# Small products on zeros, a quartered input and a later residual at the head of a two-layer trunk

## The chip, the cores and the metric

The kernel runs on one core of a Trainium2 chip. Its time is the device time of one execution in microseconds (us); the metric is the median over several runs. A core has TensorE (PE: matrix products, with PEld as its weight loads), VectorE (DVE), ScalarE (ACT), GpSimd (POOL) and SyncE (SP, which only issues transfers here).

## The reference, cut to what matters

Two layers work on 256 prompt rows and 32 sample rows (8 batches of 4), each of 1024 features. A layer is a feed-forward half step, a mixing step and a second feed-forward half step, each followed by a residual sum and a layer norm:

```python
def swiglu(x, w_in, w_out):
    gate, up = jnp.split(x @ w_in, 2, axis=-1)
    return (jax.nn.silu(gate) * up) @ w_out
...
x = layer_norm(ALPHA * x + 0.5 * swiglu(x, p['ffn1_w_in'][l], p['ffn1_w_out'][l]), p['ln1_g'][l], p['ln1_b'][l])
z = x @ p['mix_w_in'][l]
...
x = layer_norm(ALPHA * x + mix, p['ln2_g'][l], p['ln2_b'][l])
x = layer_norm(ALPHA * x + 0.5 * swiglu(x, p['ffn2_w_in'][l], p['ffn2_w_out'][l]), p['ln3_g'][l], p['ln3_b'][l])
```

`ffn1_w_in` has 1024 rows and 2 x 2816 columns. Everything is float32. The mixing step (three groups of heads) is not touched by the change.

## The kernel before

All activations are held with features on the 128 partitions and the 288 tokens along the row: x is eight chunks of 128 x 288. To keep float32 accuracy on a faster form of product, each operand is split into a high part (rounded to the format that PE takes at full pace) and a low part (the rest), and a product is three: low weights by high x, high weights by high x, high weights by low x.

`load_x` (line 720) brings the input in. It comes in rows of tokens, in three tiles `xin` (128, 128 and 32 rows of 1024 features), each in two halves of the features, all issued by SP; after the loads of each half it calls `prep` for one block of weights. Then, for each of the eight chunks, PE transposes the three pieces into one PSUM tile `xps`, ACT makes the high part, DVE the low part, and ACT a copy times ALPHA into `ax`, the tile in which the residual sum is formed at the end of the feed-forward step.

`prep` (line 338) loads a block of up to four chunks by 256 columns (`raw`, three buffers), lets ACT make its high part `wh` and DVE its low part `wl` (three buffers each), with a priority of 250 instructions ahead of what was traced before. `weights` (line 359) keeps up to two blocks prepared ahead in the list `wr`. `dense_g` (line 390) forms one product of 256 columns from the blocks that `blocks` lists (chunks 0 to 3, then 4 to 7 for the 1024 features); `block` (line 374) issues the three products of each chunk, for two column halves: 24 products a block, 48 for 256 columns.

`ffn` (line 465) goes through eleven rounds, each a gate product and an up product of 256 columns; before round j it calls `mid[j]()`: in layer 0 the constants made on POOL (`consts`, round 0) and the small parameters (`params`, rounds 5 and 6). `post` (line 496) adds the output product to `ax` and forms the norm. The order of each engine's instructions comes from a scheduler that works by these priorities and by what is ready in its own model of time, so an instruction may stand well ahead of the place where the program has it; on the chip each engine takes its instructions in that fixed order, and so does SP its transfers.

Of the kernel before, what the change touches and what calls it, by code (L numbers as in the profile page):

```python
# [8 lines left out]
F32 = mybir.dt.float32  # L9
F32R = mybir.dt.float32r  # L10
BF16 = mybir.dt.bfloat16
# [6 lines left out]
DM = 1024  # L18
T = 256
# [19 lines left out]
class Trunk:  # L39
    def __init__(self, ctx, tc, I, O):  # L40
# [12 lines left out]
        self.dn, self.dshare, self.l = 0, False, 0  # L53

# [27 lines left out]
    @contextmanager  # L82
    def prio(self, n):
        """Work that the scheduler may issue ahead of what is traced before it."""
        v = PR.get(n, 0) + PR.get(f"{n}@{self.l}", 0)
        self.tc.cur_priority -= v
        yield
        self.tc.cur_priority += v
# [31 lines left out]
    def consts(self):  # L120
# [34 lines left out]
        # causal masks over [s, t]: t > s and t >= s  # L155
# [5 lines left out]
        # block-merge masks: ml[b][t, s] and mt[b][s, t]  # L161
# [13 lines left out]
        # the same for blocks of 64 tokens, in rows of (block parity, token)  # L175
# [19 lines left out]
        # sample block masks over [(h,s), (h,t)], blocks of four tokens  # L195
# [9 lines left out]
        # the same with the rows of head h at the place of head (h + 2) % 4  # L205
# [3 lines left out]
        # row -> batch within a 32-token group, and row -> parity of its head  # L209
# [10 lines left out]
        # sums over a head's 64 rows into 32 equal rows, and their spreading back  # L220
# [11 lines left out]
        # a token's row in each group of 32; minus one at odd rows  # L232
# [3 lines left out]
        # two heads' inclusive sample blocks in either half of the rows  # L236
# [17 lines left out]
        # a token's row in each group of 32, for either pair of heads  # L254
# [3 lines left out]
        # the first four rows repeated for each batch  # L258
# [3 lines left out]
        # token -> batch, and a token's row in each group of 32  # L262
# [4 lines left out]
        # reset points of the running sums: token 0 of each chunk  # L267
# [70 lines left out]
    def prep(self, spec):  # L338
        """A block of weights, loaded and split into high and low parts."""
# [19 lines left out]
    def weights(self, spec):  # L359
        """The prepared block; the next one in line is prepared before it is used."""  # L360
        if not self.wq or self.wq[0] != spec:
            return self.prep(spec)
        while len(self.wr) < 2 and len(self.wr) < len(self.wq):
            self.wr.append(self.prep(self.wq[len(self.wr)]))
        self.wq.pop(0)
        return self.wr.pop(0)
# [7 lines left out]
    def block(self, spec, x, res, first, last):  # L374
        """A block's share of a product."""
# [14 lines left out]
    def dense_g(self, w, n0, x, nk, pool, res):  # L390
        res += [self.dps() for _ in range(2)]
        bl = self.blocks(w, n0, nk, pool)
# [9 lines left out]
    def dense_by(self, w, n0s, x, groups):  # L402
        """Several products, each group of chunks through all of them before the next."""
# [7 lines left out]
    def fill(self, n=1):  # L411
        """Goes on with the products in the background by n steps."""
# [18 lines left out]
    def hilo(self, r, name, n=NT):  # L431
        """Rows of high and low parts in turn, of equal rows."""
# [5 lines left out]
    def newx(self, nt):  # L438
        """Operand tiles of a product's moving side: eight 128-row chunks, high and low parts."""
# [9 lines left out]
    def zfix(self, ps, st, nm):  # L449
        """A product's two column blocks, and their biases, with the norm's scale (and shift) applied."""  # L450
# [45 lines left out]
    def post(self, wout, x, nk, coef, ln, shift, groups=None):  # L496
        """Residual sum with a product, and its layer norm: the operand tiles of the next product hold
        (u - m) g in high and low parts, with m the mean of the first six chunks (shift) or of all."""
# [100 lines left out]
    def final(self, po, m6, coef, g, square, i):  # L599
        """The last norm, in rows of tokens, and the outputs; the last rows are the prompt's end and the samples."""  # L600
# [6 lines left out]
        def rows(j, c):  # L607
            """A chunk, times the norm's gain, in rows of tokens."""
# [40 lines left out]
        # the mean's rest as rows of high, low and high parts  # L649
# [34 lines left out]
    def final_load(self, l):  # L684
        """The last norm's shift in each row, and its gain in (negated) rows of high, high and low parts."""
# [10 lines left out]
    def residual_g(self, pend):  # L696
        """The norm's output itself, times ALPHA for the next residual sum."""
# [9 lines left out]
    def residual_x(self):  # L707
        """The same, and operand tiles of it."""
# [11 lines left out]
    def load_x(self, specs):  # L720
        """The operand tiles of the inputs; both loads in halves of the features, and the first weights between."""
        nc, I = self.nc, self.I
        rows = []
        xin = [self.m4([128, DM], f"xin{j}") for j in range(3)]
        self.wq += specs
        for hf in range(2):
            fs = slice(512 * hf, 512 * hf + 512)
            for j, r in enumerate(xin):
                if j < 2:
                    nc.sync.dma_start(r[:, fs], I["x_prompt"][0, j * 128:(j + 1) * 128, fs])  # L730
                else:
                    nc.sync.dma_start(r[:NS, fs], I["x_sample"].rearrange("b t d -> (b t) d")[:, fs])
            self.wr.append(self.prep(specs[hf]))
        x = self.newx(NT)
        for c in range(KC):
            p = self.ps(f"xps{c}")
            for j, r in enumerate(xin):
                n = 128 if j < 2 else NS
                self.tr(p[:, 128 * j:128 * j + n], r[:n, c * 128:(c + 1) * 128])
            self.act(x[0][c], p[:, :NT])  # L740
            self.sub(x[1][c], p[:, :NT], x[0][c].bitcast(F32))
            self.act(self.ax[:, c], p[:, :NT], scale=ALPHA)
        return x

# [43 lines left out]
    def rw_pre(self, l, q, zs):  # L788
# [3 lines left out]
        # lora products  # L792
# [3 lines left out]
        else:  # L796
            # tanh(x) = 2 sigmoid(2 x) - 1
# [19 lines left out]
        # running sums of the log decay (in units of -exp(-0.5)), centred in each chunk  # L817
# [17 lines left out]
        # keys  # L835
# [30 lines left out]
        # (sum r k r_k) v, and the norm's shift  # L866
# [13 lines left out]
    def gnorm(self, l, x, n):  # L880
        """Rows of tokens, less the means of n groups of 64, and one over each group's deviation."""
# [12 lines left out]
    def rw_gate(self, q, OT, p, G, BO, m, ts):  # L894
        """The norm's gain and shift, the bonus and the gate, into chunks 0 and 1 of the operand tiles m."""
# [33 lines left out]
    def rw_prompt(self, l, KR, bh, kh, V, eP, em):  # L929
        """Four chunks of 64 tokens; rows are (chunk parity, token), matrices [rows, chunk pair, head, token]."""  # L930
# [8 lines left out]
        # token-major values, first keys beside AT[1] in the order of its matrices, second keys  # L939
# [15 lines left out]
        def heads(j=None, i=None):  # L955
            """Chunk pair, parity, head pair, head, its rows, its columns and its matrix."""
# [7 lines left out]
        def pairs(name, f):  # L964
            """Products of both head parities, in turn in the array's two row halves."""
# [9 lines left out]
        for qi, src in ((0, bh), (2, kh)):  # L975
# [13 lines left out]
            if qi == 0:  # L989
                # the inverse over pairs of tokens, and its transpose  # L990
# [12 lines left out]
        # token-major values, keys and (negated) first operands  # L1003
# [15 lines left out]
        # inverses over twice as many tokens, from I - (the block between two halves) times the inverse  # L1019
# [25 lines left out]
        # corrections without the state, and their dependence on it  # L1045
# [11 lines left out]
        # from one chunk's state to the next, and to the outputs  # L1057
# [3 lines left out]
        # decay from a chunk's centre to its end, and on to the next chunk's centre  # L1061
# [36 lines left out]
        # token-major outputs  # L1098
# [31 lines left out]
    def rw_load(self, l):  # L1130
        nc, I = self.nc, self.I
        # carried states, rows (parity of the batch, value)
# [7 lines left out]
    def rw_sample(self, l, KR, bh, kh, V, eP):  # L1140
# [9 lines left out]
        # the carried states transposed to rows (head, key)  # L1150
# [8 lines left out]
        # keys and queries of each batch alone  # L1159
# [508 lines left out]
    def run(self):  # L1668
# [6 lines left out]
        def par(l):  # L1675
            return lambda: q.append(self.params(l))
# [156 lines left out]
```

## Time and profile before

| | us |
|---|---|
| median of 3 runs | 1374.07 |
| the three runs | 1373.8, 1374.07, 1381.42 |
| span of the profiled execution | 1379.8 |

The profiled execution's span is the time from its first to its last instruction on the core; PE is busy 1308.3 us of it (95%), DVE 1009.8, ACT 663.8, POOL 274.1. Matmuls are pipelined, so a busy PE is not one at its full pace: the distance between the starts of two products tells the pace. A row of the trace names the engine, the line of the kernel and the tiles (out <- in); "x7" means that seven such instructions are merged, and the time in front of it is from the first start to the last end. What stands in square brackets is the engine's idle time before the row and what ended it. "d" is the PSUM tile of the dense products, "xps" that of the transposes.

### The profile page before, as it was taken

What the parts mean: (1) busy time and instruction counts of PE and PEld (TensorE: products, weight loads), DVE (VectorE), ACT (ScalarE), POOL (GpSimd) and SP (SyncE); (2) the same over time, 40 slices, a digit from 0 to 9 for tenths busy, and PEclk for the clock granted to TensorE, in tenths of its full rate; (3) what the DMA queues carried; (4) which work ended last, traced back from release to release, by engine and by line L of the source; (5) the groups of instructions that cost most, each with busy time, mean ns of one, the idle gap of its engine ahead of it and who ended that gap; (6) DMA issues with size and microseconds to landing.
All of it is one profiled execution on the core that took longest, in us unless ns stands there. A gap on an engine that the chain in (4) does not pass through costs nothing.

```text
span 1379.8 us, 27635 instructions
## 1 busy us (share of the span) xinstructions
PE 1308.3 (95%) x11161; PEld 1255.1 (91%) x11162; DVE 1009.8 (73%) x1844; ACT 663.8 (48%) x1052; POOL 274.1 (20%) x381
## 2 busy tenths in 40 slices
PE   7999999898987999999999999998889889999998
PEld 6999999877876999999999999997778789999997
DVE  3555448977877998774698775599986889977643
ACT  4454435762345554443465443368333645544433
POOL 9200001435554100000100000033464421000002
PEclk9999999987997999999999999999999889999999
DMA  5655554531123655554455555554212544555551
GB/s 175 187 168 168 162 165 150 154 106 34 48 86 113 187 156 158 165 168 153 155 168 167 167 156 161 167 160 131 78 31 71 149 124 145 168 161 161 175 168 58
DMA packets 208158, 194.12 MB, mean 141 GB/s; under 512 B 15911, under 2 KB 206363, under 8 KB 208030
## 3 DMA queue, kind: packets, MB, share of 16 engines
q1 hardware_dynamic: 207326, 190.91, 44.9%
q0 software_dynamic: 608, 1.31, 0.4%
q8 instruction: 88, 1.44, 0.4%
q14 instruction: 40, 0.33, 0.1%
q10 hardware_dynamic: 96, 0.13, 0.1%
HBM read 185.10 MB, written 7.22 MB: 139 GB/s over the span
## 4 chain that ended last, share of the span: by engine, by line
PE 79%; DVE 14%; issue 3%; ACT 2%; POOL 1%; DMA 0%; POOLq 0%; SPq 0%; DVEq 0%; ACTq 0%
PE d L97 71%; DVE wl L65 2%; DVE hgO L77 1%; ACT wh L62 1%; DVE yrw L77 1%; DVE hgQ L77 1%; PE pA L97 1%; DVE hR L65 1%; DVE hAT L94 1%; PE hO L97 0%; PE hA L97 0%; DVE ax L65 0%; PE pD L97 0%; POOL hgP L65 0%; DVE hL L65 0%
## 5 line engine op out<-in xcount | busy, mean ns | idle before, releaser
L97 PE MATMUL d<-x,wh 128*128 128x290 f32 (+1 forms) x3968 | 824.0, 301 | 2.5 <-DVE x L77 2.5
L97 PEld LDWEIGHTS d<-x,wh 128*128 128x128 f32 x3968 | 653.3, 192 | 9.8 <-DVE x L77 4.3
L97 PE MATMUL d<-x,wl 128*128 128x290 f32 (+1 forms) x1984 | 602.5, 304 | 16.2 <-ACT x L62 12.4
L62 ACT ACTIVATE wh<-raw 128x1024 fp32r<-128x1024 f32 x344 | 357.2, 1039 | 456.1 <-PE d L97 312.1
L65 DVE TENSOR_TENSOR wl<-raw,wh 128x1024 fp32r<-128x1024 f32 x324 | 395.1, 1220 | 239.4 <-ACT wh L62 238.1
L97 PEld LDWEIGHTS d<-x,wl 128*128 128x128 f32 x1984 | 380.5, 192 | 21.5 <-ACT x L62 15.5
L97 PE MATMUL d<-h,wh 128*128 128x288 f32 x1408 | 282.0, 296 | 0.0
L97 PEld LDWEIGHTS d<-h,wh 128*128 128x128 f32 x1408 | 226.2, 188 | 0.2
L97 PE MATMUL d<-h,wl 128*128 128x288 f32 x704 | 207.8, 295 | 0.0
L65 POOL TENSOR_TENSOR lnv<-lnq,lnq 128x288 f32<-128x288 f32 x6 | 8.2, 1375 | 848.7 <-ACT lnq L62 848.7
L97 PEld LDWEIGHTS d<-h,wl 128*128 128x128 f32 x704 | 132.5, 188 | 0.2
L65 POOL TENSOR_TENSOR wl<-raw,wh 128x1024 fp32r<-128x1024 f32 x20 | 50.0, 2502 | 66.3 <-ACT wh L62 66.3
L62 ACT ACTIVATE h<-sg 128x288 fp32r<-128x288 f32 x88 | 38.1, 435 | 24.5 <-DVE sg L65 20.9
L62 ACT ACTIVATE sg<-yg,ccg 128x288 f32<-128x288 f32 x66 | 34.3, 528 | 29.9 <-DVE yg L77 29.9
L62 ACT ACT_TABLE_LOAD x37 | 47.5, 1283 | 1.4 <-PEq L1821 0.8
L65 DVE TENSOR_TENSOR h<-sg,h 128x288 fp32r<-128x288 f32 x88 | 39.6, 452 | 5.6 <-ACT h L62 5.6
L77 DVE SCALAR_TENSOR_TENSOR ax<-d,ax 128x288 f32<-128x288 f32 x48 | 21.4, 452 | 29.4 <-PE d L97 29.4
L77 DVE SCALAR_TENSOR_TENSOR yu<-nu,ccu,yu 128x288 f32<-128x288 f32 x66 | 33.9, 514 | 0.8
L77 DVE SCALAR_TENSOR_TENSOR yg<-nu,ccg,yg 128x288 f32<-128x288 f32 x66 | 33.8, 515 | 0.8
L62 ACT ACTIVATE lnq<-ax 128x288 f32<-128x288 f32 x48 | 20.9, 435 | 26.2 <-DVE ax L77 26.0
L77 DVE SCALAR_TENSOR_TENSOR sg<-yu,ccu,sg 128x288 f32<-128x288 f32 x66 | 33.3, 509 | 0.0
L65 DVE TENSOR_TENSOR yu<-d,rho 128x288 f32<-128x288 f32 x66 | 29.5, 448 | 0.0
(499 smaller groups left out, 1355.2 us busy)
## 6 DMA issues: line engine op xcount, KB each, us to landing
raw<-in_ffn_w_in SPq DMA_DIRECT2D x176, 512.0 KB
raw<-in_ffn_w_out SPq DMA_DIRECT2D x80, 512.0 KB
raw<-in_mix_w_in SPq DMA_DIRECT2D x56, 512.0 KB
raw<-in_mix_w_out SPq DMA_DIRECT2D x12, 512.0 KB
raw<-in_ffn_w_out SPq DMA_DIRECT2D x16, 256.0 KB
hs<-in_state_hgrn SPq DMA_DIRECT2D x8, 512.0 KB
out_hgrn_state_sample<-hs SPq DMA_DIRECT2D x8, 512.0 KB
raw<-in_mix_w_out SPq DMA_DIRECT2D x8, 256.0 KB
```

The costliest lines, as they stand in the source:

```text
L62: self.nc.scalar.activation(out, in_, func, **kw)
L65: (eng or self.nc.vector).tensor_tensor(out, a, b, op=op)
L77: self.nc.vector.scalar_tensor_tensor(out, a, s, b, op0=op0, op1=op1)
L94: self.nc.vector.copy_predicated(out, mask.bitcast(I16), data)
L97: self.nc.tensor.matmul(out, lhsT, rhs, start=start, stop=stop)
```

## The change

Five things are changed. PE gets 14 products (128 x 128 by 128 x 288, 16-bit) on a tile of zeros before anything else, into a PSUM tile that nobody reads. The prompt's x is loaded in quarters of the features, both 128-row tiles in one transfer, by SP; the samples' quarters are issued by ACT. The first weight column is loaded in three blocks (chunks 0 and 1, 2 and 3, 4 to 7) in place of two, one after each of the first three quarters, and `dense_g` takes that list for the first product. The ACT copies times ALPHA are gone from `load_x`. In their place `residual_0`, called before round 4 of the first feed-forward step, adds the high and the low part of each chunk on POOL into `ax` and scales it by ALPHA on ACT. The rest of the diff takes away comments and is left out here.

```diff
-        self.dn, self.dshare, self.l = 0, False, 0
+        self.dn, self.dshare, self.l, self.head = 0, False, 0, None
...
     def dense_g(self, w, n0, x, nk, pool, res):
         res += [self.dps() for _ in range(2)]
-        bl = self.blocks(w, n0, nk, pool)
+        bl, self.head = self.head or self.blocks(w, n0, nk, pool), None
...
-    def load_x(self, specs):
+    def load_x(self, w):
         nc, I = self.nc, self.I
-        rows = []
-        xin = [self.m4([128, DM], f"xin{j}") for j in range(3)]
-        self.wq += specs
-        for hf in range(2):
-            fs = slice(512 * hf, 512 * hf + 512)
-            for j, r in enumerate(xin):
-                if j < 2:
-                    nc.sync.dma_start(r[:, fs], I["x_prompt"][0, j * 128:(j + 1) * 128, fs])
-                else:
-                    nc.sync.dma_start(r[:NS, fs], I["x_sample"].rearrange("b t d -> (b t) d")[:, fs])
-            self.wr.append(self.prep(specs[hf]))
+        wt = self.ep.tile([128, NT], BF16, tag="e", name="warm", bufs=B["e"])
+        nc.vector.memset(wt, 0.0)
+        p = self.ps("warmps")
+        for _ in range(WARM):
+            self.mm(p[:, :NT], wt[:, 0:128], wt)
+        xp = [self.m4([128, 2, 512], f"xin{j}") for j in range(2)]
+        xs = self.m4([128, DM], "xins")
+        ks = ((0, 1), (2, 3), tuple(range(4, 8)))
+        self.head = [(*w, k, 0, False) for k in ks]
+        self.wq += self.head
+        for f in range(4):
+            fs = slice(256 * f, 256 * f + 256)
+            nc.sync.dma_start(xp[f // 2][:, :, 256 * (f % 2):256 * (f % 2) + 256],
+                              I["x_prompt"][0, :, fs].rearrange("(j p) f -> p j f", p=128))
+            nc.scalar.dma_start(xs[:NS, fs], I["x_sample"].rearrange("b t d -> (b t) d")[:, fs])
+            if f < 3:
+                self.wr.append(self.prep(self.head[f]))
         x = self.newx(NT)
         for c in range(KC):
             p = self.ps(f"xps{c}")
-            for j, r in enumerate(xin):
-                n = 128 if j < 2 else NS
-                self.tr(p[:, 128 * j:128 * j + n], r[:n, c * 128:(c + 1) * 128])
+            for j in range(2):
+                self.tr(p[:, 128 * j:128 * j + 128], xp[c // 4][:, j, 128 * (c % 4):128 * (c % 4) + 128])
+            self.tr(p[:, T:NT], xs[:NS, c * 128:(c + 1) * 128])
             self.act(x[0][c], p[:, :NT])
             self.sub(x[1][c], p[:, :NT], x[0][c].bitcast(F32))
-            self.act(self.ax[:, c], p[:, :NT], scale=ALPHA)
+        self.x0 = x
         return x
 
+    def residual_0(self):
+        ax = self.ax
+        for c in range(KC):
+            self.add(ax[:, c], self.x0[0][c].bitcast(F32), self.x0[1][c].bitcast(F32), self.nc.gpsimd)
+            self.act(ax[:, c], ax[:, c], scale=ALPHA)
...
-        x, st = self.load_x(self.blocks(("ffn1_w_in", 0), 0, KC)), None
+        x, st = self.load_x(("ffn1_w_in", 0)), None
...
-                mid = {0: self.consts, 5: par(0), 6: par(1)}
+                mid = {0: self.consts, 4: self.residual_0, 5: par(0), 6: par(1)}
...
+WARM = 14
```

## Rows read from the trace of the kernel before

**Rows 1.** Busy time by stage: PE, PEld, DVE, ACT, POOL, granted clock, DMA share, GB/s

```profile
0.00:21.00 21.00, 14.05 (x52) 10.47 (x53) 6.33 (x10) 8.54 (x16) 19.22 (x73) 1.00 0.65 208
21.00:215.00 194.00, 194.00 (x1456) 193.76 (x1457) 99.88 (x152) 87.56 (x130) 21.70 (x72) 1.00 0.53 166
...
240.00:480.00 240.00, 212.10 (x2289) 188.79 (x2289) 192.45 (x369) 121.09 (x223) 104.97 (x112) 0.89 0.35 103
```

**Rows 2.** Chain of waits that ended last, its head: start us, us, what

```profile
2.19 6.02 DMA raw<-in_ffn_w_in
...
9.31 1.24 DVE wl L65
...
10.69 2.03 PE d L97 x7
...
15.37 5.10 PE d L97 x20
...
20.96 60.51 PE d L97 x453
```

**Rows 3.** Timeline of PE in the head: start us, us, engine, line, tiles, count

```profile
4.08 0.45 PE L101 MATMUL xps<-ident,xin 128*128 128x128 f32 x1 [4.08 <-DMA xin<-in_x_prompt]
4.72 3.30 PE L101 MATMUL xps<-ident,xin 128*128 128x128 f32 x11 [0.19 <-DMA xin<-in_x_prompt]
...
12.72 2.65 PE L101 MATMUL xps<-ident,xin 128*128 128x128 f32 x9
15.30 0.85 PE L97 MATMUL d<-x,wh 128*128 128x288 f32 x2
...
19.55 0.68 PE L97 MATMUL d<-x,wh 128*128 128x288 f32 x2
20.03 0.44 PE L97 MATMUL d<-x,wl 128*128 128x288 f32 x1
20.27 0.69 PE L101 MATMUL xps<-ident,xin 128*128 128x128 f32 x3
20.89 0.54 PE L97 MATMUL d<-x,wh 128*128 128x288 f32 x2
```

**Rows 4.** Transfers by line, with the size of each

```profile
raw<-in_ffn_w_in SPq DMA_DIRECT2D x176, 512.0 KB
...
xin<-in_x_prompt SPq DMA_DIRECT2D x4, 256.0 KB
```

**Rows 5.** Timeline of ACT, in the head and at the kernel's end

```profile
8.23 1.06 ACT L62 ACTIVATE wh<-raw 128x1024 fp32r<-128x1024 f32 x1 [6.14 <-DMA raw<-in_ffn_w_in]
...
11.30 1.06 ACT L62 ACTIVATE wh<-raw 128x1024 fp32r<-128x1024 f32 x1 [1.12 <-DMA raw<-in_ffn_w_in]
...
13.14 1.07 ACT L62 ACTIVATE wh<-raw 128x1024 fp32r<-128x1024 f32 x1
...
1374.31 1.11 ACTq L682 DMA_DIRECT2D out_y_sample<-yout  x2
```

**Rows 6.** Timeline of POOL: the constants' end and its next work

```profile
37.89 0.13 POOL L763 MEMSET Z<- 128x1 f32 x2
...
219.78 1.51 POOL L65 TENSOR_TENSOR lnv<-lnq,lnq 128x288 f32<-128x288 f32 x1 [175.78 <-ACT lnq L62]
221.37 4.09 POOL L65 TENSOR_TENSOR lnv<-lnv,lnq 128x288 f32<-128x288 f32 x4
```

**Rows 7.** Groups of instructions from 10 to 20.2 us, PE alone: busy us, mean ns

```profile
L97 PE MATMUL d<-x,wl 128*128 128x288 f32 x10 | 4.6, 456 | 2.7 <-DVE wl L65 2.7
```

**Rows 8.** Busy time in stretches of 2 us after a pause of PE

```profile
260.00:262.00 2.00, 0.45 (x4) 0.21 (x2) 2.00 (x2) 0.00 (x0) 1.72 (x1) 1.00 0.86 142
262.00:264.00 2.00, 0.00 (x0) 0.00 (x0) 2.00 (x8) 1.84 (x4) 0.81 (x4) 0.72 0.79 263
...
268.00:270.00 2.00, 2.00 (x10) 1.68 (x10) 0.88 (x7) 1.20 (x2) 0.00 (x0) 0.57 0.85 261
```

**Rows 9.** Waits of ACT from 21 to 215 us, the longest

```profile
ACT wh L62 <- PE d L97: 61.6, 35, 4.0
```

## The prediction

> **What bounds the kernel now.** I read the granted clock of the core and the windows by stage first. TensorE (PE) is busy 194.00 of 194.00 us in the first feed-forward stretch (21 to 215), but only 14.05 of the first 21 [rows 1]. So a microsecond won before 21 reaches 215 whole, where PE alone holds the time. The mixing stretches have holes (PE 212.10 of 240 us, mean clock 0.89 in the first [rows 1]); the change touches nothing there.
>
> The chain of waits tells what the first 21 us wait for: the first weights' transfer (6.02 us to its landing), their split on ACT and DVE, 7 products, 9 transposes of x, 20 products, 3 transposes, and from 20.96 products alone [rows 2, 3]. The PE timeline gives the pace. Products start 0.24 us apart before 20.27 (19.55 to 20.03 for two) and from 20.96 on run at 60.51/453 = 0.1336 us; 288 columns in 0.24 us is the lower level, 1.2 GHz [rows 2, 3]. The granted clock stands at 1.00 for the whole head [rows 1], so it misses this first low stretch; I go by the spacing. Twelve transposes ran from 4.08 to 8.02 and did not end it; it ended some 5 us into an unbroken run of products [rows 3].
>
> My milestone is the 48th product, the last of the first 1024x256 weight column: 27 had started by 20.96, so 21 x 0.1336 later, at **23.77 us**. What the change gains is 23.77 less its own time for the same 48 products and 24 transposes.
>
> **The change part by part.**
>
> *Loads.* Before, SP queues 576 KB of x (two times 256 and 64), 512 of weights, 576, 512 [rows 4] (the samples' part, 32 rows of 512 numbers, is 64 KB). The second tile of x was there at 4.72, the weights at 8.23 and 11.30 [rows 3, 5]: queue positions 512, 1088 and 2176 KB. I read the new order off this line. The 128 KB of samples go from ACT's queue early, so they stand in front: weights of chunks 0 and 1 end at 256 + 256 + 128 = 640 KB, 5.5 us; the second x quarter at 896, 7.1; chunks 2 and 3 at 1152, 8.4; the third quarter at 1408, 9.1; the last weights at 1920, 10.6; the last quarter at 2176, 11.3. The first quarter is one 256 KB transfer like the tile that landed at 4.08 [rows 3]; I take 4.3. SP issues seven transfers instead of eight (and one more block of weights) ahead of those that wait for a buffer: no cost. ACT issues four, at 1.11/2 = 0.56 us, so 2.2 us, in a stretch where it idles now: 6.14 us, to 8.23 [rows 5].
>
> *Small products on zeros.* One DVE fill, which I let end at 1.2 (DVE's first work of before is at 9.31 [rows 2]), then 14 products of 288 columns. No row shows this bf16 form at the low level. Bounds: 14 x 0.1336 = 1.9 us (over by 3.1), and 14 x 0.456, the full length of a low product with no overlap [rows 7], 6.4 us (over by 7.6). I take the spacing 0.24, the nearest row: 3.36 us, over by **4.56**. They stand where PE waits for x. The lower bound gains nothing, since no product can start before 7.1; by the upper one the first two chunks' transposes end at 9.3, over 2 us behind that.
>
> *Splits.* The weights of chunks 0 and 1 are half a block; half of 1.06 on ACT and 1.24 on DVE [rows 2, 5] is some 0.55 and 0.65 (bounds: the half and the whole, which would be 1.1 us later). Behind the first chunks' copies that is 5.9 to 6.4 and 6.4 to 7.1: first product at **7.1** instead of 10.69. The last block lands at 10.6, then 1.06 + 1.24 and 0.14 of handing over (9.31 + 1.24 to 10.69) [rows 2, 5]: not before **13.1**.
>
> *PE's work.* A chunk's three transposes take (15.30 - 12.72)/3 = 0.86 us low and 20.89 - 20.27 = 0.62 at the rise [rows 3]. If the clock stayed low: chunks 0 and 1 to 6.28, wait to 7.1, 12 products to 9.98, two chunks to 11.70, 12 products to 14.58, four chunks (3.44) and 24 products (5.76) to **23.78**. That is the number of before to 0.01: the earlier loads alone give nothing, since PE fills the time with low-clock work. All hangs on when the clock rises. If it rises at the end of the first burst (9.98), what is left costs 6 x 0.62 + 36 x 0.1336 = 8.5, end 18.5, gain 5.3. At the end of the second (14.58): 4 x 0.62 + 24 x 0.1336 = 5.7, end 20.3, gain 3.5. Midway **4.4 us**. For a rise in a stretch that is not unbroken there is a row: within 268 to 270 the clock goes up (mean 0.57) while PE's weight loads are busy 1.68 of 2.00 us [rows 8].
>
> *Residual later.* Eight ACT copies leave the head; none stands on the chain [rows 2]. Eight POOL additions and eight ACT scalings come in at the fifth of eleven rounds. POOL's additions of this shape take 1.0 to 1.5 us (4.09/4, 1.51) [rows 6], 8 to 12 us, and POOL is idle from 44 to 219.8 [rows 6]; ACT is busy 87.56 of 194 [rows 1]. Nothing at this cover; without it, see the slower rival.
>
> *Next in line.* The fourth weight block now waits for the split of the first half block (7.1) instead of 10.5; its queue position, 2688 KB, is where the third block of before stood, split from 13.14 on [rows 5]. Split from there it is ready at 15.5, before any end above. Hidden.
>
> **The transpose rule.** The row: 12 transposes in a row, 3.9 us, left PE at the lower level [rows 3]. The Trainium skill, TensorE: Matmul & The Clock Gate, Part 4, says why it could matter here: a transpose does not count as PE being busy in the way a product does, so the full clock does not engage on it; the trace agrees. By it this change, which sets transposes between bursts of products, would hold the clock down: that is the second rival, and the sum would be 1.4 us or less instead of 4.4.
>
> **The rivals.**
>
> *The zeros do it all.* The clock rises with them, near 4.6, and stays. Then the data bound: 13.1 + 24 x 0.1336 = 16.3, plus up to 0.5 for the last chunk's split behind the weights' on DVE; gain 7.0 to 7.5, time 1366.8. For: 3.4 us of unbroken products. Against: they end at 4.56 and the next come at 7.1; PE was busy for the first 0.45 us of 260 to 262, then stopped, and the clock was down within 262 to 264 (a mean of 0.72, so from about 262.9) [rows 8].
>
> *The clock rises as late as before.* Transposes break each burst of 2.9 us. Low to 20.5, with 23.78 - 20.5 = 3.3 us of low work left, done in 1.8: 22.3, gain 1.4; low to the end, gain 0. Time 1373.4. The change's first part then does not do what it says. For: the 9 transposes of before, after which it took 5 us more [rows 3].
>
> *Slower than before: ACT held by POOL.* ACT takes its queue in order, and behind a residual scaling stand the high parts of weights, for which DVE and then PE wait. POOL works without a break to 44, and work that comes later in the program (a fill of Z at 37.89) already stands ahead of its last constants [rows 6]; so scalings may stand early in ACT's queue. If ACT comes to them at 55 and waits for eight additions, 12 us, PE loses that less its lead of one block, 24 x 0.1336 = 3.2: 8.8, less the gain 4.4, time 1378.5. If ACT comes to them at 25, it is held to 44 + 12 = 56, PE loses 27.8, time 1397.5. It is slower by over 1% from a hold of 21 us. Against: in 21 to 215 ACT's waits for PE sum to 61.6 us [rows 9], so the splits have room.
>
> **How the numbers follow.** The profiled execution spans 1379.8 us, above the median of the three runs, 1374.07, and inside their 1373.8 to 1381.42; against its own time the forecast is 1379.8 - 4.4 = 1375.4, and against the median 1369.7. Chances: rise during the first bursts 0.45 (1369.7, from 1368.8 to 1370.6), zeros do it all 0.22 (1366.8), rise as late as before 0.23 (1373.4), held ACT 0.10 (1378.5 and up). Runs of one kernel lie up to 7.6 us apart, so I blur each case by some 3 us. The range takes in all but the slower rival's far end and the fast edge: 1363 to 1377. About 1%, 13.7 us, is what a measurement of this kernel can tell from no change. Faster by over 1% needs 1360.3, nearly twice the largest gain worked out above: 0.04. Slower by over 1%, 1387.8, needs the long hold: 0.03. Within 1%: 0.93.
>
> **What would show it.** The first product on x near 7 us (before 10.69); the first spacing of 0.13 us between 10 and 15; the 48th product near 19 to 20; the next weights split before PE asks; PE full from there to the first norm, now near 211. The forecast is wrong if products keep 0.24 us beyond 17, if the first product waits for more than its own quarter (then it starts near 9), if PE idles for weights between 14 and 60, or if the mixing stretches change length by more than the gain.

## The result and the profile after

The changed kernel takes 1390.89 us (median of 6 runs, 1390.07 to 1398.98) against 1374.26 for the kernel before (6 runs, 1373.54 to 1381.75): ratio 1.0113, interval 1.0081 to 1.0144. It is 16.6 us slower; 1369.7 was forecast, with a range to 1377. Executions of the kernel before fall into two groups, 1372 to 1377 and 1378 to 1384 (one run of 1438.16 stands apart), so a median, which can jump from one to the other, is read here with the ratio (close to that of the means) and with the stages of a profile beside it.

The profiled execution of after spans 1390.3 us. Its windows by stage (columns as in [rows 1]):

```profile
0.00:21.00 21.00, 15.13 (x63) 10.49 (x64) 6.85 (x13) 7.51 (x13) 19.04 (x76) 0.76 0.56 183
21.00:215.00 194.00, 183.88 (x1377) 183.65 (x1377) 93.85 (x144) 85.54 (x129) 21.05 (x77) 0.97 0.51 158
```

The stretch that was full before, 194.00 of 194.00 us [rows 1], now has a hole of 10.1 us on PE. The chain of waits of after shows where it lies (start us, us, what); the line at 226.46 is the output product at the first norm, my second landmark, and the last line the next feed-forward step, behind the mixing stage:

```profile
36.52 1.52 POOL ax L65 x2
38.41 1.05 ACT wh L62
39.48 1.24 DVE wl L65
40.76 52.37 PE d L97 x384
...
226.46 14.09 PE d L97 x106
...
526.45 158.97 PE d L97 x1190
```

The same two pieces in before:

```profile
215.15 14.11 PE d L97 x106
...
518.59 159.53 PE d L97 x1190
```

So 11.31 us are lost by the first norm (12.46 against another profiled execution of before, e0 below). In front of the hole the chain now runs through POOL, which before was on it nowhere in the head [rows 2]. The timelines of the four engines tell the rest. ACT of after, in the head and from 21 us:

```profile
5.54 0.63 ACT L62 ACTIVATE wh<-raw 128x512 fp32r<-128x512 f32 x1 [1.42 <-DMA raw<-in_ffn_w_in]
7.13 0.63 ACT L62 ACTIVATE wh<-raw 128x512 fp32r<-128x512 f32 x1 [0.96 <-DMA raw<-in_ffn_w_in]
10.10 1.06 ACT L62 ACTIVATE wh<-raw 128x1024 fp32r<-128x1024 f32 x1 [2.33 <-DMA raw<-in_ffn_w_in]
11.06 1.29 ACT L62 ACTIVATE x<-xps 128x288 fp32r<-128x288 f32 x4
...
21.15 1.06 ACT L62 ACTIVATE wh<-raw 128x1024 fp32r<-128x1024 f32 x1 [0.78 <-PE d L97]
33.60 0.44 ACT L62 ACTIVATE ax<-ax 128x288 f32<-128x288 f32 x1 [11.38 <-POOL ax L65]
...
38.06 0.44 ACT L62 ACTIVATE ax<-ax 128x288 f32<-128x288 f32 x1 [0.30 <-POOL ax L65]
38.41 1.04 ACT L62 ACTIVATE wh<-raw 128x1024 fp32r<-128x1024 f32 x1
```

POOL of after; `L152` makes constants, `ax<-x,x` is the residual's addition:

```profile
24.73 0.52 POOL L152 TENSOR_SCALAR_AFFINE_SELECT bd<-bd 128x128 bf16<-128x128 bf16 x1
...
32.77 0.79 POOL L65 TENSOR_TENSOR ax<-x,x 128x288 f32<-128x288 f32 x1
33.52 0.21 POOL L65 TENSOR_TENSOR b<-b 128x4 f32<-128x4 f32 x1
...
36.49 3.04 POOL L65 TENSOR_TENSOR ax<-x,x 128x288 f32<-128x288 f32 x4
```

DVE and PE of after:

```profile
39.48 1.23 DVE L65 TENSOR_TENSOR wl<-raw,wh 128x1024 fp32r<-128x1024 f32 x1 [15.99 <-ACT wh L62]
```

```profile
1.14 3.54 PE L97 MATMUL warmps<-warm 128*128 128x288 bf16 x14 [1.14 <-DVE warm L725]
4.85 0.66 PE L101 MATMUL xps<-ident,xin 128*128 128x128 f32 x2 [0.17 <-DMA xin<-in_x_prompt]
...
6.39 0.44 PE L101 MATMUL xps<-ident,xin 128*128 128x128 f32 x2
...
7.30 0.24 PE L101 MATMUL xps<-ident,xins 32*128 32x32 f32 x1
11.50 0.61 PE L97 MATMUL d<-x,wl 128*128 128x288 f32 x1 [3.96 <-ACT x L62]
...
23.86 0.43 PE L97 MATMUL d<-x,wh 128*128 128x288 f32 x2
...
40.76 0.61 PE L97 MATMUL d<-x,wl 128*128 128x288 f32 x1 [10.12 <-DVE wl L65]
```

Two things are to be seen. First, ACT came to the first scaling at 22.2 us and waited 11.38 us, since POOL, busy with constants, made the first addition only at 32.77. I call this wait the hold. Behind six of the eight scalings in ACT's queue stood the split of the next weights, at 38.41; DVE's part followed at 39.48, and PE, through at 30.6 with the products whose weights were ready, waited 10.12 us. The granted clock fell with the pause: the record of it shows 0.50 from 33.4 to 43.6, so the 2.8 us of products from 40.76 on ran at 1.2 GHz and cost another 1.4. Sum 11.5, against 11.31 at the landmark.

Second, the head gained nothing. ACT's queue had all three splits of weights ahead of the first copy of x. The third one's transfer came at 10.10, though the first four chunks had been transposed by 7.5; the first product stood at 11.50 instead of 10.69 [rows 2], and the 48th near 24.0 instead of 23.77.

### The profile page after: what moved, and what is told of

It is laid out like the page before. It is cut to its first block, busy times and chain, and to the rows that moved or that the text cites. A ratio compares the mean times of both kernels' runs of the same rounds, so it can differ in the third digit from the quotient of the medians.

```text
span 1390.3 us, 27678 instructions
## 1 busy us (share of the span) xinstructions
PE 1311.2 (94%) x11176; PEld 1256.2 (90%) x11176; DVE 1011.0 (73%) x1846; ACT 664.6 (48%) x1053; POOL 276.4 (20%) x389
## 4 chain that ended last, share of the span: by engine, by line
PE 77%; DVE 13%; POOL 4%; issue 3%; ACT 2%; SPq 0%; DMA 0%; POOLq 0%; DVEq 0%; ACTq 0%
PE d L97 69%; DVE wl L65 2%; DVE hgO L77 1%; ACT wh L62 1%; PE pA L97 1%; DVE hR L65 1%; DVE hgQ L77 1%; DVE ax L65 1%; PE hA L97 1%; PE hO L97 0%; POOL hgP L65 0%; PE pD L97 0%; DVE yo L77 0%; DVE hL L65 0%; POOL mt L152 0%
## 5 line engine op out<-in xcount | busy, mean ns | idle before, releaser
L65 DVE TENSOR_TENSOR wl<-raw,wh 128x1024 fp32r<-128x1024 f32 (+1 forms) x325 | 395.0, 1216 | 245.6 <-ACT wh L62 244.6
L62 ACT ACTIVATE wh<-raw 128x1024 fp32r<-128x1024 f32 (+1 forms) x345 | 357.3, 1036 | 448.0 <-PE d L97 305.9
L65 POOL TENSOR_TENSOR lnv<-lnq,lnq 128x288 f32<-128x288 f32 x6 | 8.2, 1372 | 858.0 <-ACT lnq L62 858.0
L77 DVE SCALAR_TENSOR_TENSOR sg<-yu,ccu,sg 128x288 f32<-128x288 f32 x66 | 33.4, 510 | 0.0
```

Source lines behind the costliest of these rows:

```text
L62: self.nc.scalar.activation(out, in_, func, **kw)
L65: (eng or self.nc.vector).tensor_tensor(out, a, b, op=op)
L77: self.nc.vector.scalar_tensor_tensor(out, a, s, b, op0=op0, op1=op1)
```

## The experiments

One table for all. "Norm" is the start of the first norm's output product in the profiled execution, "mixing" the time from there to the 1190 products of the next feed-forward step, both from the chain of waits; "profiled" is that execution's own time. The median of before beside each set of runs: 1373.99 (e1 to e4), 1374.53 (e0, e5 to e7), 1380.61 (e8, e9), 1374.60 (e10; 1374.46 without the run of 1438.16). e0 to e7 ran on one chip, e8 and e9 on a second, e10 and e11 on two more, each beside before on the same chip.

| kernel | median (range; runs) | ratio (interval) | norm | mixing | profiled |
|---|---|---|---|---|---|
| before | see above | | 215.15 | 303.44 | 1381.42 |
| e0 before again | 1374.39 (1372.60-1382.56; 10) | 1.0004 (0.9980-1.0027) | 214.00 | 293.97 | 1372.78 |
| after | 1390.89 (1390.07-1398.98; 6) | 1.0113 (1.0081-1.0144) | 226.46 | 299.99 | 1392.0 |
| e2 residual alone | 1393.43 (1393.20-1395.95; 4) | 1.0132 (1.0079-1.0185) | 228.76 | 300.10 | 1393.21 |
| e1 copies in the head | 1383.26 (1374.97-1386.12; 10) | 1.0030 (1.0002-1.0058) | 215.31 | 303.63 | 1385.68 |
| e3 POOL scales | 1383.42 (1373.51-1385.13; 10) | 1.0041 (1.0012-1.0069) | 214.84 | 302.40 | 1382.63 |
| e4 e3 without zeros | 1381.69 (1372.61-1387.24; 10) | 1.0043 (1.0011-1.0074) | 214.61 | 295.96 | 1378.67 |
| e5 e3, copies first | 1377.43 (1370.87-1380.73; 10) | 0.9994 (0.9968-1.0019) | 210.34 | 299.89 | 1375.70 |
| e9 e5 again | 1375.53 (1371.04-1380.70; 12) | 0.9971 (0.9948-0.9995) | 210.06 | 300.37 | 1375.63 |
| e8 e5, more zeros | 1380.53 (1371.39-1382.18; 12) | 1.0001 (0.9974-1.0028) | 213.09 | 302.72 | 1381.59 |
| e10 e8, weights behind | 1371.62 (1370.02-1378.89; 12) | 0.9977 (0.9953-1.0001) | 208.33 | 303.45 | 1378.79 |
| e11 e10 again | one run, 1379.30 | | 208.37 | 303.39 | 1379.30 |
| e6 before, shift of 8 | 1383.97 (1379.62-1386.45; 10) | 1.0055 (1.0036-1.0075) | 214.67 | 303.00 | 1382.06 |
| e7 before, shift of 16 | 1383.35 (1375.42-1389.13; 10) | 1.0054 (1.0025-1.0083) | 216.06 | 303.59 | 1383.36 |

**The later residual, alone and undone.** Theory: ACT's wait for POOL costs the time up to the first norm. Rival: the new loads or the zeros do. e2 puts the later residual alone into the kernel before; e1 is the whole change with the copies times ALPHA back in the head; e3 is the whole change, but POOL scales what it has added, so that nothing of the residual is in ACT's queue.

```diff
 # e1, against after
+            self.act(self.ax[:, c], p[:, :NT], scale=ALPHA)
-                mid = {0: self.consts, 4: self.residual_0, 5: par(0), 6: par(1)}
+                mid = {0: self.consts, 5: par(0), 6: par(1)}
 # e2, against before (residual_0 as in the change)
-            self.act(self.ax[:, c], p[:, :NT], scale=ALPHA)
+        self.x0 = x
-                mid = {0: self.consts, 5: par(0), 6: par(1)}
+                mid = {0: self.consts, 4: self.residual_0, 5: par(0), 6: par(1)}
 # e3, against after
-            self.act(ax[:, c], ax[:, c], scale=ALPHA)
+            self.ts(ax[:, c], ax[:, c], ALPHA, None, ALU.mult, ALU.bypass, self.nc.gpsimd)
```

> The whole change but its last part: the copies times ALPHA are made by ACT from PSUM inside the input step, as before, and nothing is added before round 4. Theory A (ACT held behind POOL's additions, 11.4 us in the changed kernel's trace, PE idle 10.1): the hold is gone, time 1390.9 less 11 to 17, so 1374 to 1380. Theory B (the loss is in the loads, the blocks or the zeros): stays at 1386 or more.

> The kernel before with only the later residual (POOL adds, ACT scales, before round 4). Theory A: ACT comes to the scalings near 24 and waits for POOL to some 33 to 36; PE idles 8 to 11 us; time 1382 to 1391. Theory B: 1374 within 2.

> The whole change, but POOL scales by ALPHA itself behind its additions, so that ACT has no scaling in its queue. Theory A: ACT's queue never waits for POOL; time 1374 to 1380, as with the copies in the head, or up to 2 less since eight copies are off ACT. Theory B: 1386 or more. If the additions themselves disturb (DVE slowed beside POOL), it stays 3 or more above the kernel with the copies in the head.

Waits of e2 between 21 and 215 us (us in total, times, longest):

```profile
ACT ax L62 <- POOL ax L65: 14.3, 3, 13.4
...
PE d L97 <- DVE wl L65: 12.1, 1, 12.1
```

and the longest of e3:

```profile
DVE wl L65 <- ACT wh L62: 78.6, 51, 2.9
```

With the old loads and no zeros, e2 has the same hold, somewhat longer (13.4 us), and the norm at 228.76, 13.6 us behind before. Without the hold, in e1 and e3, PE waits for no weights and the norm is back at 215.31 and 214.84. So the hold is the cause of the 11.3 us, and the loads and zeros are not. The times alone would not have told the theories apart: e1 and e3, at 1383, lie between the 1374 to 1380 of the one and the 1386 of the other, and e2 is 2 us over its range. By their medians e1 and e3 are still 9 us above before, 0.3 to 0.4% by their ratios, with the norm in the same place. That part lies behind the norm (below).

**The head: the zeros, and the order on ACT.** e4 is e3 without the zeros. e5 is e3 with an order made by hand: as the prediction had it on ACT and DVE, the copies of chunks 0 and 1 ahead of the second block's split, those of 2 and 3 ahead of the third's; and on PE the 24 products of the first two blocks ahead of the transposes of chunks 4 to 7. e9 is e5 once more.

```diff
 # e4, against e3
-WARM = 14
+WARM = 0
 # e5, against e3: a split comes behind the last copies made (a on ACT, b on DVE)
+                    if c:
+                        es.enter_context(self.tc.issue_after(a.ins))
+                        es.enter_context(self.tc.issue_after(b.ins))
+                    self.parts(self.head[i], raw, hi, lo)
...
+                if last is not None:
+                    es.enter_context(self.tc.issue_after(last.ins))
                 for j in range(2):
                     self.tr(...)
```

> As the kernel where POOL scales, without the 14 products on zeros. If the clock that they raise is lost again before the first product on x (the changed kernel's trace: up from 6.0 to 9.5, the first product at 11.5), the time is the same within 1.5 us. If the zeros carry the head, it is 3 to 6 us longer.

> The whole change with POOL scaling, and with the order that the prediction took for granted: on ACT and DVE the copies of chunks 0 and 1 stand ahead of the split of the second block, those of 2 and 3 ahead of the third block's, and on PE the 24 products of the first two blocks ahead of the transposes of chunks 4 to 7. If ACT's queue (the third block's split, waiting for its transfer to 9.3 to 10.3 us, ahead of copies that were ready near 5) is what held the first product to 11.5, the first product is at 7 to 8 us and the last product of the first feed-forward stretch (first at 214.8 where POOL scales) starts at 210 to 213.5. If the transfers or the clock set it, 214 to 215.5.

Without the zeros the norm is at 214.61, with them (e3) at 214.84: here they are worth nothing, though the medians are 1.7 us apart, just over the 1.5 expected. The clock that they were to raise, and that rose in after (two transposes in 0.44 us from 6.39), did not rise in e3 at all, whose transposes stay at the low pace:

```profile
7.00 0.69 PE L101 MATMUL xps<-ident,xin 128*128 128x128 f32 x2
```

Nor did it in e1, e5 and e9, with the same 14 zeros: 0.69 us for two transposes, and products 0.24 us apart until 13.5 (e9) to 20.7 (e3). What tells is the pace of PE; the record of the granted clock shows 1.00 there, as it did in the head of before. In e5 ACT takes the copies between the splits, and PE's first product comes at 8.61; ACT and then PE of e5:

```profile
4.96 0.63 ACT L62 ACTIVATE wh<-raw 128x512 fp32r<-128x512 f32 x1 [0.84 <-DMA raw<-in_ffn_w_in]
5.50 0.39 ACT L789 ACTIVATE x<-xps 128x288 fp32r<-128x288 f32 x1
...
10.24 1.06 ACT L62 ACTIVATE wh<-raw 128x1024 fp32r<-128x1024 f32 x1 [1.11 <-DMA raw<-in_ffn_w_in]
```

```profile
7.75 0.69 PE L101 MATMUL xps<-ident,xin 128*128 128x128 f32 x2
8.37 0.31 PE L101 MATMUL xps<-ident,xins 32*128 32x32 f32 x1
8.61 0.61 PE L97 MATMUL d<-x,wl 128*128 128x288 f32 x1
...
13.57 0.43 PE L773 MATMUL d<-x,wh 128*128 128x288 f32 x1
13.81 0.33 PE L97 MATMUL d<-x,wl 128*128 128x288 f32 x1
13.98 0.29 PE L97 MATMUL d<-x,wh 128*128 128x288 f32 x1
```

Products start 0.24 us apart to 13.8 and 0.13 from there, and the norm is 4.5 us earlier than in e3, 4.8 earlier than in before (3.7 than in e0). So the order of the instructions had cost the head its gain; e5 sets it on three engines at once, and what ACT's share of that is alone was not run. On PE the transposes of four chunks still stand ahead of the first product. The second run of the same kernel:

> The kernel of e5 once more, beside e8 and the kernel before. If its 4.8 us at the head reach the end whenever the mixing stages run as in before's quickest executions, its lowest times stay 1 to 4 us under before's lowest (1372); its median is within 5 us of before's, and what lies between goes by the share of executions in which the mixing stages take 6 to 9 us more. If the head's gain were given back for good, its lowest times would equal before's.

Its norm is at 210.06 again. Its lowest time, 1371.04, is 0.8 us under before's lowest beside it (1371.82), its median 5.1 under a median of before that was itself 6 us higher in that set (13 of 23 runs in the upper group). By the ratio e9 is just clear of no change and e5 is not. So the head's gain is seen in both profiles, and that it reaches the end is not shown.

**Zeros that keep the clock.** In e5 PE runs transposes alone from 4.48 to 8.6, and the clock is low when products begin. e8 puts four more zero products behind the transposes of each of chunks 0, 1 and 2; e10 then puts the splits of the weights that follow behind the last four chunks' copies.

```diff
 # e8, against e5
+                t = nc.tensor.transpose(p[:, T:NT], xs[:NS, c * 128:(c + 1) * 128], self.ident[:NS, :NS])
+            if c < 3:
+                with ExitStack() as es:
+                    es.enter_context(self.tc.issue_after(t.ins))
+                    for _ in range(4):
+                        zl = nc.tensor.matmul(pz[:, :NT], wt[:, 0:128], wt, start=True, stop=True)
 # e10, against e8: in load_x, and at the next split in prep
+        self.hold = [a.ins, b.ins]
...
+            for i in self.hold:
+                es.enter_context(self.tc.issue_after(i))
```

> The kernel of e5 (copies ahead of the splits, POOL scales itself), with four more products on zeros behind the transposes of each of the chunks 0, 1 and 2, so that PE doesn't pause and doesn't run transposes alone between the first zeros and the first product on x. In e5 the first product starts at 8.6 us, products are 0.24 us apart to 13.8, and the first norm's output products start at 210.3. Theory that the clock which the zeros raise near 6 us can be carried over: products 0.13 us apart from the first one on, which comes at 9 to 10; 24 of them end near 12.5 instead of 14.3, and the norm's products start 1.0 to 2.5 us earlier, at 208 to 209.3. Rival, transposes among short bursts of products don't hold the clock: products 0.24 us apart to near 14 as in e5, started up to 1.5 us later, and the norm's products at 210.3 to 212. The median then goes by which group of times the mixing stages fall into, 1370 to 1380 either way.

> The kernel of e8 (copies ahead of the splits, zeros between the first chunks' transposes), with the splits of the weights that follow the head (the fourth block and on) put behind the copies of the last four chunks on ACT and DVE. In e8 these splits stood ahead of the copies; ACT waited for their transfers to 11.87 and 15.41 us, PE for the copies to 16.82, the clock fell, and the norm's products came at 213.1 although the first 24 products had ended at 11.8. Theory (the order on ACT alone cost e8 its gain, and the clock raised by zeros can be kept): products 0.13 us apart throughout, the last four chunks transposed by 14.0, the 48th product near 17.5, the norm's products at 207 to 209, 1 to 3 us earlier than in e5. Rival (with the head that fast, weights become the bound): PE waits for DVE's split of the fourth or fifth block between 17 and 25 us, and the norm's products come at 209 to 212. The time: lowest runs 1368 to 1370.5 by the theory, 1370 to 1373 by the rival; the median 2 to 6 us under before's, if the mixing stages fall into their groups as often as in e5.

> The kernel of e10 once more, for the profile of another execution of it. Its head ends 5.7 us before that of the quickest execution of before that was profiled (first norm's products at 208.3 against 214.0), yet its lowest time is only 2 us lower. If the head's gain is lost in the mixing stages, an execution near 1371 has the norm's products again at 208 to 209 and takes 3 to 5 us more than that execution's 294.0 in the first mixing stage or 264.7 in the second, with more of the low clock there. If it is lost ahead of them, the norm's products come at 211 to 213. An execution near 1379 has the first mixing stage at 302 to 304 again.

ACT of e8, and PE of e8 with the wait that followed:

```profile
11.87 1.06 ACT L62 ACTIVATE wh<-raw 128x1024 fp32r<-128x1024 f32 x1 [1.20 <-DMA raw<-in_ffn_w_in]
15.41 1.06 ACT L62 ACTIVATE wh<-raw 128x1024 fp32r<-128x1024 f32 x1 [2.48 <-DMA raw<-in_ffn_w_in]
16.37 1.29 ACT L797 ACTIVATE x<-xps 128x288 fp32r<-128x288 f32 x4
```

```profile
8.52 0.40 PE L97 MATMUL d<-x,wl 128*128 128x288 f32 x1
8.76 0.29 PE L97 MATMUL d<-x,wh 128*128 128x288 f32 x1
...
13.75 0.24 PE L791 MATMUL xps<-ident,xins 32*128 32x32 f32 x1
...
16.82 0.61 PE L97 MATMUL d<-x,wl 128*128 128x288 f32 x1 [1.85 <-ACT x L797]
```

The clock was up: products 0.13 us apart from 8.76 on, 24 of them done by 12. Then the same fault as in after cost more than had been won over e5, which neither side of the expectation had: two splits stood ahead of the last copies and waited for their transfers; PE paused, the clock fell, and products ran 0.24 us apart from 16.82 to 22.7. The norm came at 213.09. e10 mends that order alone; its PE:

```profile
6.97 0.67 PE L799 MATMUL warmps<-warm 128*128 128x288 bf16 x4
...
8.95 0.40 PE L97 MATMUL d<-x,wl 128*128 128x288 f32 x1
9.19 0.30 PE L97 MATMUL d<-x,wh 128*128 128x288 f32 x1
...
14.17 0.24 PE L794 MATMUL xps<-ident,xins 32*128 32x32 f32 x1
14.34 0.40 PE L97 MATMUL d<-x,wl 128*128 128x288 f32 x1
```

PE waits for nothing from 9 to 215 us, and the norm is at 208.33 (208.37 in e11), 6.8 us earlier than in before and 5.7 earlier than in e0. e10 has the lowest median here, 1371.62 against 1374.46 beside it, though its interval just reaches no change and by the ratio it is level with e9. Of 6 to 7 us at the head, 2 to 3 show in its median and lowest time. e11 was to find the rest in an execution near 1371, but it fell at 1379.3, with the first mixing stage again at 303.4. Where the quick executions lose the rest stays open. For the profiled ones the traces show it: e10 and before are alike in the first mixing stage (303.45 and 303.44), but the second, from 885.08 (before 892.80) to the products of the next feed-forward step, takes 267.6 us in e10 and 266.4 in e11 against 262.8, at a mean granted clock of 0.92 and 0.91 against 0.94, and e11 takes 1.9 us more behind it.

**A shift alone.** What of the 16.6 us lies behind the norm? The suspicion was that the stages behind the norm take another time when they start later. e6 and e7 are the kernel before with 8 and 16 products more in the ninth round of the first feed-forward step (1.1 and 2.1 us at 0.13; they add work, and nobody reads them). e0 is the kernel before, untouched.

```diff
 # e6, against before (range(16) in e7)
+            if l == 0 and j == 8 and win[0] == "ffn1_w_in":
+                p = self.ps("shift")
+                for k in range(8):
+                    self.mm(p[:, :NT], x[0][k % 8][:, 0:128], x[0][k % 8])
```

> The kernel before, unchanged, under its own name: shows how far the median of one kernel moves. If the executions fall into two or three groups by the clock of the mixing stages alone, its runs lie near 1373, 1378 and 1381 as the ones before do, and its trace has the first norm's product at 215.2 within 2 us.

> [...] If the mixing stages' clock pattern is a matter of chance, the groups stay and the median is 1.1 above that of before, some 1375 with most runs near 1374. If it hangs on where the stages lie against the start, the groups change: most runs then lie 5 to 9 above.

> [...] By chance: 2.1 above before, most runs near 1375 to 1376. If the place against the start counts: other groups than with 8.

e0 is at 1374.39, and e6 and e7 at 1383.97 and 1383.35: with 1 or 2 us of work more they are 9 above before by the median, 0.55% by the ratio. The profiles differ behind the norm, at one place above all. A window of 35 us from some 80 us behind the norm, in e0:

```profile
294.00:329.00 35.00, 28.38 (x465) 23.55 (x463) 33.07 (x73) 12.04 (x29) 18.39 (x18) 0.95 0.25 77
```

in before:

```profile
295.00:330.00 35.00, 32.37 (x362) 25.96 (x360) 22.93 (x56) 9.68 (x22) 13.20 (x15) 0.66 0.20 61
```

in after:

```profile
306.00:341.00 35.00, 32.25 (x394) 26.12 (x394) 24.12 (x57) 9.43 (x23) 14.80 (x16) 0.71 0.20 62
```

and in e6:

```profile
294.00:329.00 35.00, 32.38 (x306) 26.26 (x304) 22.81 (x55) 9.47 (x22) 13.15 (x15) 0.66 0.20 62
```

The mean granted clock there is 0.95 in e0 and 0.66 to 0.71 in the others. In the record it is one unbroken stretch of low clock, of 20.5 us in after, e2, e5 and e9, and of 23.9 in all others but e0 and e4, which have none of that length. The mixing column follows: 294 to 296 without it, 300 with the shorter, 302 to 304 with the longer. So 6 us of after's distance to e0 go with this stretch. It comes by execution: the same program gave e0's 293.97 and before's 303.44. How often it comes differs by kernel, if the times are its measure: none of e6's ten runs and two of e7's are under 1379, where before and e0 have 28 of 41 in the same set. That the place of the stages against the start decides it is not shown. The norms of e6 and e7, 214.67 and 216.06, lie 0.5 us before and 0.9 behind before's, whose own two profiles are 1.15 apart; and e1, e3 and e4 have medians 8 to 9 above before with the norm between 214.61 and 215.31. What decides it stays open, and so does why the set of before on the chip of e8 and e9 had most runs in the upper group.

## Why the prediction was wrong, point by point

*Loads, and the length of the zeros: right.* The first weights' split began at 5.54 (5.5 said), the second, earlier than said, at 7.13 (8.4), the third at 10.10 (10.6); the zeros ended at 4.68 (4.56). The fourth block's split was hidden, as said, though it waited for PE until 19.31, where 13.14 was said.

*Splits: the step that lost the head's gain.* "Behind the first chunks' copies" the first split was to be followed by the first product at 7.1. That took an order on ACT for granted: the scheduler put all three splits ahead of any copy, and the product came at 11.50. Splits go 250 instructions ahead of what was traced before them; the step should have asked what stands in front of the copies. e5 gives ACT and DVE that order: 8.6 us, a clock that rises at 13.8, inside the 9.98 to 14.58 foreseen, and 4.8 us against before (3.7 against e0) where 4.4 were said. That the sizes are so near is in part luck, for PE's order was taken for granted too: the prediction has 12 products behind the first two chunks, and after and e5 have four chunks' transposes there, which, with a wait of 0.68 us for the second quarter of x, is why e5 starts at 8.6 and not at 7.1. The mechanism of the head was right, on queues that the change didn't have.

*When the clock rises.* The rival "zeros do it all" was priced at 7.0 to 7.5 with the argument against it that PE stops between 4.56 and 7.1. In after the clock rose near 6.1 by the transposes' pace, and in a longer pause, PE standing still from 7.5 to 11.5, it fell: the record has 0.50 from 9.5 to 19.7. In e1, e3, e5 and e9 the same zeros did not raise it, though PE's work up to 6 us was nearly the same; why after's alone did is open. With 12 zeros more between the transposes it was up in e8, e10 and e11, and e10 shows that the price was near: with no wait on ACT the head gains 5.7 to 6.8. For transposes the row was [rows 3]; e5 adds four chunks' transposes, from 4.48 to 8.6 with a pause of 0.7 us, behind 3.3 us of zeros, and the clock was low at their end. The Trainium skill, TensorE: Matmul & The Clock Gate, Part 4, says that a transpose does not count as busy time of PE as a product does; e5 and e8, which differ in the zeros between the transposes, agree with it (products 0.24 us apart at first in the one, 0.13 in the other).

*Residual later: the step that decided.* "Nothing at this cover" rested on POOL's idle time from 44 on and ACT's share of 87.56 in 194 us [rows 1, 6], as if the scalings stood where the program has them, at the fifth of eleven rounds. The last part of x that they need was ready at 17.75 us (DVE's, behind ACT's copy from 16.85). ACT came to them at 22.2, while POOL was still making constants, and a busy share says nothing of what is queued behind an instruction that waits. The slower rival had this mechanism, its place (ACT at 25) and the same victims, with 0.10 of the chance; only its size was off. It had the additions behind all constants, to 56, and 27.8 us lost. POOL took them among the last constants from 32.77 at 0.80 us each, where 1.0 to 1.5 was read off [rows 6], and PE lost 11.5, so the term that the prediction put at nothing was 11.3 us at the norm. Before itself had the sign: a fill that comes later in the program stood ahead of POOL's last constants [rows 6]. From that row more of the chance belonged to this rival. The prediction's own sign for it came true: PE idled for weights between 14 and 60.

*"The change touches nothing there".* The work of the mixing stages is untouched, their time is not. Against e0's execution, after's has 12.5 us more to the norm and 6.0 more in the first mixing stage, which is nearly all of the 19.2 between the two. The slower rival's threshold, a hold of 21 us for 1%, was worked out without this second part, with the head's gain of 4.4 taken off and with no low clock behind the pause; a hold of 11.4 was enough. The prediction knew that runs of one kernel lie 7.6 us apart and took that for scatter around the median. It is a stage with two or three lengths, and the median turns from one to another when a kernel has one of them more often.

## What to carry to other kernels

When an operation is moved to another engine, ask first how early a scheduler may place it, which is as early as its operands are ready, and what stands behind it in each queue when its producer is late: here six scalings of 0.44 us, waiting for POOL, held weights that had room to spare. Zeros in front paid nothing by themselves (e3 against e4); with more of them between the transposes and no pause behind, the norm came 2.0 us earlier (e10 against e5). So fix the order on the engine that feeds PE first (e5), then bridge (e8), and look at the next order again (e10). Judge the clock at the start by the spacing of products, since here the record missed the low stretch. And where the executions of a kernel come in groups, compare landmarks in the trace, not medians alone, for any part that is worth less than the distance of the groups.

## What the runs showed of the hardware

Products on zeros can raise the clock as products on data do. In after two transposes take 0.66 us at 4.85 and 0.44 from 6.39, behind 14 zeros that ended at 4.68. The same zeros did not do so in e1, e3, e5 and e9, where two transposes stay at 0.69. With 26 of them the products of e8, e10 and e11 run 0.13 us apart from the second on.

The kernel before has one stretch, some 80 us behind the first norm, that runs at a mean clock of 0.95 or of 0.66 in different executions; its mixing stage takes 293.97 us in the one and 303.44 in the other. With 1.1 us of work added ahead of it (e6) the median was 9.4 us higher (1383.97 against 1374.53). No run here explains the choice.
